# Sample score products grouped under a priority of their own, and the first head's key and query parts a step sooner

## The chip, the cores and the metric

The kernel runs on one core of one Trainium2 chip. The time is that of one execution on the device, in microseconds (us); lower is better. Below, "before" is the kernel as it stands and "after" the changed one.

## The reference: what is computed

One layer of a hybrid decoder, in float32: a half-step SwiGLU FFN, a mixing stage, a second half-step FFN, each behind RMS norms. The mixing stage runs differential attention (four heads) and an mLSTM (four heads) side by side on the same projections. There is one prompt of 512 tokens and there are 8 samples of 4 new tokens each; the samples attend to 512 past tokens that lie in 4 pages of 128 tokens each in a paged cache.

```python
proj = h @ w_in                      # 1024 -> 3592: q, k, v of attention, q, k, v, o of the mLSTM, gates
...
past_k = cache_k[l][page_table].reshape(DB, -1, H_ATT, ATT_KDIM)
...
logits = jnp.einsum('bqhcd,bkhcd->bchqk', q, k, preferred_element_type=jnp.float32) * (ATT_DQ ** -0.5)
...
p = jax.nn.softmax(logits, axis=-1)
a = p[:, 0] - lam * p[:, 1]
return jnp.einsum('bhqk,bkhd->bqhd', a.astype(v.dtype), v)
```

For a sample, keys are the 512 past ones and the 4 new ones; each head has two logit maps (`c` is 0 or 1), whose softmaxes are subtracted.

## The kernel before

**Stages.** First FFN (to about 430 us of the span), mixing stage (about 430 to 760), second FFN. All tokens, 512 + 32, stand in the free dimension, in two halves of 288 and 256 columns, with 1024 features as 8 tiles of 128 partitions. A float32 product is done as three products of rounded parts (`mm3`, L252 to L254): weight high by input high, weight high by input low, weight low by input high. So half a projection tile is 8 x 3 = 24 matmuls of 288 or 256 columns. The rounded weight parts `wh` (ScalarE, L240) and `wl` (VectorE, L241) are made from `raw` weights just before.

**Order in the mixing stage.** `mix` writes a row of projections. `run(project(...))` takes one step of every side queue (`side.step()`) after each half projection. The queues are generators: `prep` (new heads, one at a time), `attn` (blocks of 128 queries, three at a time), `ml` and `mls` (mLSTM of prompt and samples) and `smp` (attention of the samples). The order of the code is a first plan; the Tile scheduler then orders each engine's instructions by priority, which without a statement to the contrary is the place in the code, as soon as it expects operands and buffers to be ready. `tc.high_priority(offset)` moves what is written in it ahead by `offset` places; `tc.issue_after(ins)` puts it behind `ins`. Each engine then runs its list strictly in that order, and semaphores make it wait where operands are late.

**Attention of the prompt.** `attn_head(h)` adds four blocks to the `attn` queue. A block's first step, for block 0, makes the head's key parts (`key_parts`, L1237) and the first query parts (`query_parts`, L1246): rounded high and low parts `cs` and `vb` on ScalarE (L1243, L1244, L1253) and VectorE (L1255). The next step has four score matmuls (QK, L1271, `aux<-cs,vb`), the softmax, four transposes (L1297) and the products with the values (L1303).

**Attention of the samples** (`attn_samples`). The samples come in two groups of four (`g`). For each pair of pages `p` and sample `j` two pages of keys are gathered by GpSimd (`page`, L1320, into one of 7 `pgin` buffers, AHEAD = 3 pages early); each is turned by four transposes (L1346) into a PSUM tile `smp` and copied by ScalarE into `pgT` (L1347). The PSUM pool `smp` has two buffers, and one of them, `lg`, holds the logits from the first score on, so the transposes of the next page wait for the copy of the last. `scores(p, j, kT)` (L1334) multiplies one head's 128x32 queries `qz` with 256 keys, for four heads: output columns `p*256` on, partitions `32*h` on. When two (p, j) are waiting, both are multiplied: 8 matmuls, here called a score group; there are 8 of them, 4 for each `g`. Behind the last comes `ln`, 16 matmuls with the 32 new keys (L1373, `smp<-kas,qz`), then the softmax (L1388 and before) and the transposed weights (L1392), then the values' pages. GpSimd's list also holds the mLSTM's sample state: load (L1519), a copy (L1520) and store (L1586).

**End of the stage.** L1600 is the last transpose of attention output; from it `X` is scaled (L1604), gated (L1815), rounded to `h` (L1787, with its remainder L1788 on VectorE), and the out projection's second half (L252 to L254 again) multiplies it.

Of the kernel before, what the change touches and what calls it, by code (L numbers as in the profile page):

```python
# [22 lines left out]
NS = NB * NT  # L23
# [7 lines left out]
H = 4  # L31
# [12 lines left out]
PLAIN = 6  # L44
KEEP = 8

LEAD = 3
# [157 lines left out]
class _Builder:  # L205
# [1003 lines left out]
    def attn_head(self, h, k, v, side):  # L1209
        nc = self.nc  # L1210
        hd = self.hd
        kt = hd.tile([128, 4, 128], F32, name="kt")
        vt = hd.tile([128, 4, 132], F32, name="vt")
        for qb in range(4):
            side.add("attn", self.attn_block(h, qb, self.X[:, 4 + h, :], k, vt))
            if qb < 2:
                yield
# [40 lines left out]
    def attn_block(self, h, qb, q, k, vt):  # L1258
        nc = self.nc
        wk = self.wk  # L1260
        n = (qb + 1) * 128
        if qb == 0:
            self.key_parts(k)
            self.query_parts(q[:, 0:n])
            yield
        P = []
        z = wk.tile([128, 6], F32, name="z", bufs=6)
        for c in range(2):
            ps = self.ps_tile()
            for a in range(2):  # L1270
                nc.tensor.matmul(ps[:, 0:n], lhsT=self.qt[:, 2 * a + c, :], rhs=self.ks[c][:, 0:n],  # L1271
                                 start=a == 0, stop=a == 1)
# [29 lines left out]
        for kb in range(qb + 1):  # L1302
            nc.tensor.matmul(po[:, 0:128], lhsT=aT[:, kb * 128:kb * 128 + 128], rhs=vt[:, kb, 0:128],  # L1303
                             start=kb == 0, stop=kb == qb)
# [8 lines left out]
    def attn_samples(self):  # L1313
        nc = self.nc
# [10 lines left out]
        todo = [(g, 2 * p + e, j) for g in range(2) for p in range(NPG // 2) for j in range(4) for e in range(2)]  # L1325
        ahead = [page(0, 4 * g + j, pg) for g, pg, j in todo[:AHEAD]]
        dm = self.mcv("dmask")
        for g in range(2):
            lg = self.smp.tile([128, 512], F32, name="smp")
            todo_scores = []  # L1330

            def scores(p, j, kT):
                for h in range(H):
                    nc.tensor.matmul(lg[32 * h:32 * h + 32, p * 256:p * 256 + 256], lhsT=self.qz[:, 4 * g + j, h, :],  # L1334
                                     rhs=kT[:, h, :], start=j == 0, stop=j == 3, tile_position=(0, 32 * h))
            for p in range(NPG // 2):
                for j in range(4):
# [10 lines left out]
                    if len(todo_scores) == 2:  # L1348
                        while todo_scores:
                            scores(*todo_scores.pop(0))  # L1350
                    todo_scores.append((p, j, kT))
# [16 lines left out]
            ln = self.smp.tile([128, 512], F32, name="smp")  # L1368
            while todo_scores:
                scores(*todo_scores.pop(0))  # L1370
            for j in range(4):
                for h in range(H):
                    nc.tensor.matmul(ln[32 * h:32 * h + 32, 0:NS], lhsT=self.qz[:, 4 * g + j, h, :], rhs=self.kas[:, h, :],  # L1373
                                     start=j == 0, stop=j == 3, tile_position=(0, 32 * h))
            Ls = self.pg.tile([128, PAST + NS], F32, name="Ls", bufs=1)
# [574 lines left out]
```

## Time and profile before

| | |
|---|---|
| runs | 1122.38, 1123.57, 1124.5 us; median 1123.57 |
| profiled execution | 1126.08 us, of which the span is 1123.3 |
| TensorE (PE) | 1102.2 us busy, 98% of the span |
| VectorE (DVE), ScalarE (ACT), GpSimd (POOL) | 845.0, 632.5, 125.5 us busy |
| mixing stage, 430 to 715 us | TensorE busy 277.76 of 285.00 us |

A row of the timeline has the start, the length of what it groups, engine, line and operation, output and inputs, count, and in square brackets the idle time of the engine just before and what ended it. Lengths of matmuls overlap (the next one starts before the last is through), so the time that a matmul costs is read from the difference of two starts. Rows of the timeline give the matmul's form as 128*32 where 128 rows and 32 columns of the array are used; the trace has two records for each score matmul, and for a new-key one as well.

### The profile page before, as it was taken

The page shows a single profiled execution, that of the slowest core. Times are in us where ns is not written, and L with a number is a line of the kernel's source. Part 1 is how long each engine was busy: PE and PEld are TensorE (multiplying, and loading weights), DVE is VectorE, ACT ScalarE, POOL GpSimd, SP SyncE. Part 2 cuts the span into 40 slices and gives each one's busy share as a digit, 9 for nine tenths or more (in the row PEclk, how much of TensorE's full clock was granted, in tenths as well). Part 3 has the DMA queues.
Part 4 walks back from the last instruction along what each step waited for, and adds up shares of the span by engine and source line. Part 5 has one row for each costly group of instructions (what it writes and reads, how often), then busy time and mean ns, then how long its engine had stood idle before and what let it go on. Part 6 is the DMA issues. An engine that isn't in the chain of part 4 may idle for free.

```text
span 1123.3 us, 21928 instructions
## 1 busy us (share of the span) xinstructions
PE 1102.2 (98%) x8722; PEld 1063.4 (95%) x8722; DVE 845.0 (75%) x1716; ACT 632.5 (56%) x1368; POOL 125.5 (11%) x177
## 2 busy tenths in 40 slices
PE   9999999999999999999999999989999999999997
PEld 8899999999999998899889789989999999999997
DVE  5897787878675799658675478889687888786544
ACT  5844455556455657667554467776355455555444
POOL 1000000000000133420244441000000000000000
PEclk9999999999999999999999999999999999999999
DMA  9443344224246555543355546643333333242272
GB/s 265 144 126 101 116 133 130 79 66 151 71 149 178 154 146 137 185 130 90 96 159 172 174 135 208 192 158 110 113 108 123 131 101 104 81 140 90 85 211 80
DMA packets 150038, 149.47 MB, mean 133 GB/s; under 512 B 5966, under 2 KB 139062, under 8 KB 148401
## 3 DMA queue, kind: packets, MB, share of 16 engines
q1 hardware_dynamic: 135600, 100.55, 30.1%
q0 software_dynamic: 11536, 44.88, 11.9%
q10 hardware_dynamic: 2800, 2.65, 0.8%
q8 instruction: 68, 1.11, 0.4%
q14 instruction: 34, 0.27, 0.1%
HBM read 130.08 MB, written 18.51 MB: 132 GB/s over the span
## 4 chain that ended last, share of the span: by engine, by line
PE 87%; DVE 5%; ACT 3%; DMA 2%; issue 2%; POOL 0%; DVEq 0%; POOLq 0%; ACTq 0%
PE acc L252 13%; PE acc L253 13%; PE acc L254 13%; PE acc L479 6%; PE acc L477 6%; PE acc L478 6%; PE aux L477 5%; PE aux L479 5%; PE aux L478 5%; PE smp L477 2%; PE smp L479 2%; PE smp L478 2%; DVE wl L241 1%; PE smp L1346 1%; ACT wh L240 1%
## 5 line engine op out<-in xcount | busy, mean ns | idle before, releaser
L240 ACT CAST wh<-raw 128x512 fp32r<-128x512 f32 (+2 forms) x281 | 182.9, 684 | 150.2 <-PE acc L253 72.2
L241 DVE TENSOR_TENSOR wl<-raw,wh 128x512 fp32r<-128x512 f32 (+2 forms) x281 | 208.6, 768 | 47.1 <-ACT wh L240 43.5
L252 PE MATMUL acc<-ha,wh 128*128 128x256 f32 (+1 forms) x576 | 166.4, 289 | 0.0
L253 PE MATMUL acc<-ha,wh 128*128 128x256 f32 (+1 forms) x576 | 166.0, 288 | 0.0
L254 PE MATMUL acc<-ha,wl 128*128 128x256 f32 (+1 forms) x576 | 165.5, 287 | 0.0
L252 PE MATMUL acc<-h,wh 128*128 128x256 f32 (+1 forms) x552 | 163.7, 297 | 0.0
L253 PE MATMUL acc<-h,wh 128*128 128x256 f32 (+1 forms) x552 | 160.3, 291 | 0.0
L254 PE MATMUL acc<-h,wl 128*128 128x256 f32 (+1 forms) x552 | 159.5, 289 | 0.0
L252 PEld LDWEIGHTS acc<-h,wh 128*128 128x128 f32 x552 | 104.0, 188 | 7.7 <-issue 7.1
L252 PEld LDWEIGHTS acc<-ha,wh 128*128 128x128 f32 x576 | 108.9, 189 | 0.8 <-ACT wh L240 0.6
L253 PEld LDWEIGHTS acc<-ha,wh 128*128 128x128 f32 x576 | 108.9, 189 | 0.1
L254 PEld LDWEIGHTS acc<-ha,wl 128*128 128x128 f32 x576 | 108.9, 189 | 0.0
L253 PEld LDWEIGHTS acc<-h,wh 128*128 128x128 f32 x552 | 104.1, 189 | 0.7 <-issue 0.4
L254 PEld LDWEIGHTS acc<-h,wl 128*128 128x128 f32 x552 | 103.9, 188 | 0.6 <-issue 0.4
L241 DVE TENSOR_TENSOR wl<-X,wh 128x1024 fp32r<-128x1024 f32 x48 | 58.8, 1224 | 26.3 <-ACT wh L240 26.3
L479 PE MATMUL acc<-t,wl 128*128 128x272 f32 x256 | 74.3, 290 | 0.0
L477 PE MATMUL acc<-h,wh 128*128 128x272 f32 x256 | 74.2, 290 | 0.0
L479 PE MATMUL acc<-h,wl 128*128 128x272 f32 x256 | 74.1, 289 | 0.0
L477 PE MATMUL acc<-t,wh 128*128 128x272 f32 x256 | 74.0, 289 | 0.0
L478 PE MATMUL acc<-t,wh 128*128 128x272 f32 x256 | 73.8, 288 | 0.0
L478 PE MATMUL acc<-h,wh 128*128 128x272 f32 x256 | 73.7, 288 | 0.0
L240 ACT CAST wh<-X 128x1024 fp32r<-128x1024 f32 x48 | 50.4, 1050 | 25.5 <-PE aux L478 14.8
(512 smaller groups left out, 3103.2 us busy)
## 6 DMA issues: line engine op xcount, KB each, us to landing
raw<-in_ffn_w_gate_dram SPq DMA_DIRECT2D x20, 1024.0 KB
raw<-in_w_in_dram SPq DMA_DIRECT2D x28, 512.0 KB
raw<-in_ffn_w_down_dram SPq DMA_DIRECT2D x21, 512.0 KB
rawx<-in_ffn_w_up_dram SPq DMA_DIRECT2D x8, 1024.0 KB
X<-in_ffn_w_up_dram SPq DMA_DIRECT2D x8, 1024.0 KB
raw<-in_ffn_w_down_dram SPq DMA_DIRECT2D x8, 1024.0 KB
raw<-in_ffn_w_down_dram SPq DMA_DIRECT2D x21, 384.0 KB
raw<-in_w_out_dram SPq DMA_DIRECT2D x7, 1024.0 KB
```

The lines of the kernel that those rows point to most:

```text
L240: self.nc.scalar.copy(out=high, in_=src)
L241: self.nc.vector.tensor_tensor(out=low, in0=src, in1=high.bitcast(F32), op=ALU.subtract)
L252: nc.tensor.matmul(ps, lhsT=wh, rhs=xh(k0 + k), start=st, stop=False)
L253: nc.tensor.matmul(ps, lhsT=wh, rhs=xl(k0 + k), start=False, stop=False)
L254: self.last_mm = nc.tensor.matmul(ps, lhsT=wl, rhs=xh(k0 + k), start=False, stop=sp).ins
L477: nc.tensor.matmul(ps, lhsT=wh[:, k0 + k, cs], rhs=high[:, k, :], start=st, stop=False, skip_group_check=True)
L478: nc.tensor.matmul(ps, lhsT=wh[:, k0 + k, cs], rhs=low[:, k, :], start=False, stop=False, skip_group_check=True)
L479: self.last_mm = nc.tensor.matmul(ps, lhsT=wl[:, k0 + k, cs], rhs=high[:, k, :], start=False, stop=sp, skip_group_check=True).ins
L1346: nc.tensor.transpose(ps[:, h * 128:h * 128 + 128], kp[:, h * 128:h * 128 + 128], self.ident)
```

## The change

Three edits, all in the mixing stage. (1) A pair's eight score products come as one group under `tc.high_priority(offset=AHEAD_OF)`, the later (p, j) first, with start and stop flags set to match. (2) The new-key products stand under the same priority, the heads in reverse order, and the last score group is put behind them with `issue_after`. (3) Head 0's key parts and first query parts are made in `attn_head`'s first step, with an extra `yield` behind them; block 0 of the other heads makes its own as before. The number of instructions of every engine stays as it was.

```diff
@@ -43,6 +43,8 @@
 
 PLAIN = 6
 KEEP = 8
+
+AHEAD_OF = 20000
 
 LEAD = 3
 
@@ -1211,6 +1213,10 @@
         hd = self.hd
         kt = hd.tile([128, 4, 128], F32, name="kt")
         vt = hd.tile([128, 4, 132], F32, name="vt")
+        if h == 0:
+            self.key_parts(k)
+            self.query_parts(self.X[:, 4, 0:128])
+            yield
         for qb in range(4):
             side.add("attn", self.attn_block(h, qb, self.X[:, 4 + h, :], k, vt))
             if qb < 2:
@@ -1260,8 +1266,9 @@
         wk = self.wk
         n = (qb + 1) * 128
         if qb == 0:
-            self.key_parts(k)
-            self.query_parts(q[:, 0:n])
+            if h:
+                self.key_parts(k)
+                self.query_parts(q[:, 0:n])
             yield
         P = []
         z = wk.tile([128, 6], F32, name="z", bufs=6)
@@ -1329,10 +1336,15 @@
             lg = self.smp.tile([128, 512], F32, name="smp")
             todo_scores = []
 
-            def scores(p, j, kT):
-                for h in range(H):
-                    nc.tensor.matmul(lg[32 * h:32 * h + 32, p * 256:p * 256 + 256], lhsT=self.qz[:, 4 * g + j, h, :],
-                                     rhs=kT[:, h, :], start=j == 0, stop=j == 3, tile_position=(0, 32 * h))
+            def scores(todo):
+
+                with self.tc.high_priority(offset=AHEAD_OF):
+                    for p, j, kT in reversed(todo):
+                        for h in range(H):
+                            nc.tensor.matmul(lg[32 * h:32 * h + 32, p * 256:p * 256 + 256],
+                                             lhsT=self.qz[:, 4 * g + j, h, :], rhs=kT[:, h, :],
+                                             start=j == 1, stop=j == 2, tile_position=(0, 32 * h))
+                todo.clear()
             for p in range(NPG // 2):
                 for j in range(4):
                     kT = self.pg.tile([128, H, 256], F32, name="pgT", bufs=3)
@@ -1346,8 +1358,7 @@
                             nc.tensor.transpose(ps[:, h * 128:h * 128 + 128], kp[:, h * 128:h * 128 + 128], self.ident)
                         nc.scalar.copy(out=kT[:, :, e * 128:e * 128 + 128], in_=ps.rearrange("p (h k) -> p h k", h=H))
                     if len(todo_scores) == 2:
-                        while todo_scores:
-                            scores(*todo_scores.pop(0))
+                        scores(todo_scores)
                     todo_scores.append((p, j, kT))
                     if p == 1 and j == 1:
                         vps = [page(1, 4 * g + jj, 0) for jj in range(4)]
@@ -1366,12 +1377,13 @@
                     nc.gpsimd.dma_start(out=self.o[name][0].rearrange("b t h d -> (b t) h d"), in_=dst)
                     yield
             ln = self.smp.tile([128, 512], F32, name="smp")
-            while todo_scores:
-                scores(*todo_scores.pop(0))
-            for j in range(4):
-                for h in range(H):
-                    nc.tensor.matmul(ln[32 * h:32 * h + 32, 0:NS], lhsT=self.qz[:, 4 * g + j, h, :], rhs=self.kas[:, h, :],
-                                     start=j == 0, stop=j == 3, tile_position=(0, 32 * h))
+            with self.tc.high_priority(offset=AHEAD_OF):
+                for j in range(4):
+                    for h in reversed(range(H)):
+                        mm = nc.tensor.matmul(ln[32 * h:32 * h + 32, 0:NS], lhsT=self.qz[:, 4 * g + j, h, :],
+                                              rhs=self.kas[:, h, :], start=j == 0, stop=j == 3, tile_position=(0, 32 * h))
+            with self.tc.issue_after(mm.ins):
+                scores(todo_scores)
             Ls = self.pg.tile([128, PAST + NS], F32, name="Ls", bufs=1)
             z = wk.tile([128, 6], F32, name="z", bufs=6)
             f = PAST - 128
```

The changed kernel's lines are numbered otherwise: scores L1344, transposes L1358, new-key products L1383, QK L1278, `mm3` L254 to L256, pages L1327, state load, copy and store L1531, L1532 and L1598.

On TensorE, at head 0's first QK products, before (the high and low parts of the input are called h_4314, h_4315 for the first half of the tokens and h_4621, h_4622 for the second):

```order
L254 MATMUL acc<-h_4621,wl 128x256
L1271 MATMUL aux<-cs,vb 128x128 x4
L252 MATMUL acc<-h_4314,wh 128x288
L253 MATMUL acc<-h_4315,wh 128x288
L254 MATMUL acc<-h_4314,wl 128x288
L252 MATMUL acc<-h_4314,wh 128x288
L253 MATMUL acc<-h_4315,wh 128x288
L254 MATMUL acc<-h_4314,wl 128x288
L252 MATMUL acc<-h_4314,wh 128x288
L1271 MATMUL aux<-cs,vb 128x256
```

and after:

```order
L256 MATMUL acc<-h_4314,wl 128x288
L1278 MATMUL aux<-cs,vb 128x128 x4
L1358 MATMUL smp<-base,pgin 128x128 x8
L254 MATMUL acc<-h_4621,wh 128x256
L1278 MATMUL aux<-cs,vb 128x256 x2
L255 MATMUL acc<-h_4622,wh 128x256
L256 MATMUL acc<-h_4621,wl 128x256
L254 MATMUL acc<-h_4621,wh 128x256
L255 MATMUL acc<-h_4622,wh 128x256
```

The first QK products stand now behind a whole half projection that they stood ahead of, two pages' transposes follow them at once, and the second block's follow after one projection product instead of seven.

On TensorE, at the third score group, around head 1's values (`aux<-base,v` are the transposes of the values to token order), before:

```order
L1198 MATMUL aux<-base,v 128x128 x4
L1297 MATMUL aux<-base,L 128x128 x4
L1346 MATMUL smp<-base,pgin 128x128 x4
L1334 MATMUL smp<-pgT,qz 32x256 x5
L1346 MATMUL smp<-base,pgin 128x128 x4
L1334 MATMUL smp<-pgT,qz 32x256 x3
L252 MATMUL acc<-h_4621,wh 128x256
L253 MATMUL acc<-h_4622,wh 128x256
```

and after:

```order
L1200 MATMUL aux<-base,v 128x128 x2
L1358 MATMUL smp<-base,pgin 128x128 x4
L1200 MATMUL aux<-base,v 128x128 x2
L1278 MATMUL aux<-cs,vb 128x128 x2
L1344 MATMUL smp<-pgT,qz 32x256 x8
L1278 MATMUL aux<-cs,vb 128x128 x2
L1358 MATMUL smp<-base,pgin 128x128 x4
```

The group is whole, with QK products on both sides, and no transposes of a page stand within it.

On GpSimd, at the last key pages of the second group of samples, before (`cs` is the mLSTM's sample state there):

```order
L1320 DMA pgin<-in_cache_k_dram,idx 128x512 x2
L1320 DMA pgin<-in_cache_v_dram,idx 128x512 x3
L1586 DMA out_dram<-cs 128x4x128
L1320 DMA pgin<-in_cache_v_dram,idx 128x512
L1519 DMA cs<-in_state_C_dram 128x4x128
L1520 COPY cs<-ncol 128x4x2
L1320 DMA pgin<-in_cache_k_dram,idx 128x512
L1586 DMA out_dram<-cs 128x4x128
```

and after:

```order
L1327 DMA pgin<-in_cache_k_dram,idx 128x512 x2
L1327 DMA pgin<-in_cache_v_dram,idx 128x512 x4
L1327 DMA pgin<-in_cache_k_dram,idx 128x512
L1598 DMA out_dram<-cs 128x4x128
L1327 DMA pgin<-in_cache_v_dram,idx 128x512
L1531 DMA cs<-in_state_C_dram 128x4x128
```

The last key page stands right behind the four value pages, and the store and the load of a state, with its copy, stand behind it.

In the counts of the whole stage, TensorE's list changes between projection products and other work 208 times now, 196 before; the sample softmax's transposed weights (L1392) of the first group have 63 matmuls between the last scores and themselves, 24 before; and the last attention transpose (L1600) stands 24 matmuls later among the out projection's.

## The prediction

> **What bounds the kernel now.** I read the page's first part, then its chain, then a table of windows over the mixing stage, the only stage that the change reorders.
>
> ```profile
> span 1123.3 us, 21928 instructions
> PE 1102.2 (98%) x8722; PEld 1063.4 (95%) x8722; DVE 845.0 (75%) x1716; ACT 632.5 (56%) x1368; POOL 125.5 (11%) x177
> PE 87%; DVE 5%; ACT 3%; DMA 2%; issue 2%; POOL 0%; DVEq 0%; POOLq 0%; ACTq 0%
> ```
>
> ```profile
> 430.00:450.00 20.00, 18.51 (x140) 17.34 (x140) 18.27 (x76) 15.38 (x44) 9.62 (x14) 1.00 0.66 178
> ...
> 630.00:650.00 20.00, 18.14 (x179) 15.46 (x178) 10.60 (x41) 10.01 (x30) 8.06 (x10) 1.00 0.51 158
> 650.00:715.00 65.00, 65.00 (x517) 58.08 (x516) 48.70 (x149) 41.63 (x124) 17.20 (x24) 1.00 0.57 179
> sum 285.00, PE 277.76 PEld 249.94 DVE 200.12 ACT 173.10 POOL 93.47; mean PE 39.68 PEld 35.71 DVE 28.59 ACT 24.73 POOL 13.35
> ```
>
> TensorE (the first figure behind the length) is busy 98% of the span at a granted clock of 1.00, so time is won only where it stands still, or where its own stream runs less densely than it could. It stands still for 285.00 - 277.76 = 7.24 us in this stage, a fifth of it at the start, where VectorE is busy 18.27 of 20 us, and a quarter around 640. The change removes and adds no instruction and leaves SyncE's order as it is. The 7.24 us, and what interleaving costs inside busy time, are all that it can win.
>
> **The change part by part.** First the score groups. The trace has two records for each of a group's eight products, and in the new order all of them stand side by side. On TensorE's timeline of before:
>
> ```profile
> 455.43 1.07 PE L1334 MATMUL smp<-pgT,qz 128*32 128x256 f32 x16 [0.27 <-issue]
> 456.43 0.39 PE L253 MATMUL acc<-h,wh 128*128 128x256 f32 x1
> ...
> 478.26 1.05 PE L1334 MATMUL smp<-pgT,qz 128*32 128x256 f32 x10
> 479.25 0.66 PE L1346 MATMUL smp<-base,pgin 128*128 128x128 f32 x4
> 479.83 0.63 PE L1334 MATMUL smp<-pgT,qz 128*32 128x256 f32 x6
> 480.39 0.39 PE L252 MATMUL acc<-h,wh 128*128 128x256 f32 x1
> ...
> 530.88 0.48 PE L1373 MATMUL smp<-kas,qz 128*32 128x32 f32 x32
> 531.29 0.40 PE L252 MATMUL acc<-h,wh 128*128 128x288 f32 x1
> ...
> 630.57 1.05 PE L1334 MATMUL smp<-pgT,qz 128*32 128x256 f32 x10
> ...
> 644.21 0.63 PE L1334 MATMUL smp<-pgT,qz 128*32 128x256 f32 x6
> 644.77 0.44 PE L1537 MATMUL aux<-base,sm 128*128 128x128 f32 x2
> ...
> 645.28 0.83 PE L1334 MATMUL smp<-pgT,qz 128*32 128x256 f32 x9
> ...
> 646.51 0.49 PE L1483 MATMUL aux<-vt,kt 128*128 128x130 f32 x2
> ```
>
> A whole group takes 456.43 - 455.43 = 1.00 us from its start to the next work's. The split one at 478.26 takes 0.99 and 0.56 us in its two pieces (479.25 - 478.26, 480.39 - 479.83): 0.55 more. The one at 630.57 is split in the same way, after ten. The one at 644.21 takes 0.56 and, with its 32 short new-key products, 1.23; whole it would be 1.00 and, as behind the first sample group, 531.29 - 530.88 = 0.41 for the short ones, so 0.4 more. Joined, the three give 0.55 + 0.55 + 0.4 = **-1.5**, and 0 if the transposes, once put elsewhere, pay the same two changes there; the whole groups of now follow on such neighbours at 1.00, so I take the full value.
>
> [...]
>
> Second, cuts. A group put into a projection interrupts it. The nearest row is four transposes there:
>
> ```profile
> 460.89 0.29 PE L254 MATMUL acc<-h,wl 128*128 128x288 f32 x1
> 461.24 0.66 PE L1346 MATMUL smp<-base,pgin 128*128 128x128 f32 x4
> 461.65 0.38 PE L252 MATMUL acc<-h,wh 128*128 128x288 f32 x1
> 461.87 0.30 PE L253 MATMUL acc<-h,wh 128*128 128x288 f32 x1
> ```
>
> The product behind the cut takes 0.22 us until the next instead of 0.13, 0.09 more; the entry, 0.35 from 460.89 instead of 0.13, is 0.22 more, part of which may be a wait. I take 0.17 a cut, the return and a third of the entry, between 0.09 and 0.31. In the new order of the stage TensorE changes 208 times between projection products and others, 196 before. That is six more cuts: **+1.0**, from +0.5 to +1.9.
>
> Third, head 0. Its key and query parts move one step ahead in program order, and its first scores one step back:
>
> ```profile
> 436.64 0.33 PE L1271 MATMUL aux<-cs,vb 128*128 128x128 f32 x1 [0.18 <-issue]
> ...
> 438.72 0.39 PE L1271 MATMUL aux<-cs,vb 128*128 128x256 f32 x1 [0.77 <-ACT wh L240]
> ...
> 443.19 1.07 PE L1271 MATMUL aux<-cs,vb 128*128 128x384 f32 x3 [0.46 <-DVE vb L1255]
> ```
>
> and on ScalarE's:
>
> ```profile
> 435.89 2.26 ACT L240 CAST wh<-raw 128x512 fp32r<-128x512 f32 x4
> ```
>
> ScalarE rounds four weights (2.26 us) between two sets of query parts, and TensorE's in-order stream, which has the products that need these parts in front, stands 0.18 + 0.77 + 0.46 us, with some 0.1 to 0.15 us of restart behind each (it shows as a first product that takes 0.23 instead of 0.13): about 1.7 us. In after a whole half projection stands ahead of the first scores, so that they start near 439.2, 3 us later, with the parts long ready. Block 1 then follows after one product, and waits for its query parts and the restart: I allow 0.65. Gain **-1.0**, between 0 (ScalarE's queue is only shifted, and the same weights are late) and -1.7. The 24-product step goes through the attention queue everywhere; its other heads keep the same neighbours within a few products, so I cost them at nothing: it is the projections' products that hide them, and without these one such stall is 0.5 us.
>
> Fourth, the last key page of the second sample group. TensorE's row and GpSimd's rows of the timeline:
>
> ```profile
> 640.04 0.63 PE L1346 MATMUL smp<-base,pgin 128*128 128x128 f32 x4 [1.85 <-DMA pgin<-in_cache_k_dram,idx]
> ```
>
> ```profile
> 630.36 0.79 POOL L1519 DMA_DIRECT2D cs<-in_state_C_dram  x1 [1.32 <-issue]
> 631.14 1.36 POOL L1520 COPY cs<-ncol 128x8 f32<-128x8 f32 x1
> 632.67 0.99 POOL L1320 DMA_INDIRECT pgin<-in_cache_k_dram,idx  x1 [0.16 <-issue]
> ```
>
> The piece of the chain of waits (start, length, what) that ends at those transposes:
>
> ```profile
> 632.67 7.24 DMA pgin<-in_cache_k_dram,idx
> ```
>
> The page's load stands behind a state's load and a copy on GpSimd; its buffer is free when the transposes near 630.5 are done, so it goes out 2.2 us later than it could. In after it stands right behind the four value pages and ahead of the state's store and load: out near 0.3 us behind those transposes, 1.9 us earlier. Its own transposes are wanted 6.65 us behind them instead of 7.7, as one step of other work in between is gone. By 7.24 us of landing, 0.3 + 7.24 - 6.65 = 0.9 us of the stall (2.0 with the restart) stay, and less if it lands sooner, with no state's load in front of it. I take half of that: **-1.5**, from -1.0 to -2.0. What is moved behind it, the state's load and store, has a whole sample step to its use.
>
> [...]
>
> Fifth, the end of the first sample group:
>
> ```profile
> 537.05 0.91 PE L1392 MATMUL smp<-s,Ls 128*128 128x128 f32 x6 [0.55 <-DVE s L1388]
> ```
>
> TensorE waits for the softmax of sample scores. Between these and this line stand 24 products before and 63 after (39 of 0.12 to 0.13 us each, some 4.8 us more). The wait with its restart is gone: **-0.7**, and nothing comes in its place unless the scores themselves are late; from -0.7 to 0.
>
> Sixth, what the priority costs. Groups and, through the PSUM pair they share, transposes come as soon as they can be planned, and so nearer to ScalarE's copies of the transposed pages:
>
> ```profile
> 467.96 0.66 PE L1346 MATMUL smp<-base,pgin 128*128 128x128 f32 x4 [0.42 <-ACT pgT L1347]
> ```
>
> and all copies of that line (shortest, median, longest in ns):
>
> ```profile
> L1347 ACT COPY pgT<-smp x32: 562/585/614, 445.5 to 640.7; 128x512 f32<-128x512 f32 x32
> ```
>
> The copy takes 585 ns. One such wait is there now (0.42, 0.58 with restart). For two places of after I find something ahead of the copy on ScalarE: an exponential and head parts ahead of one page's, about 0.6, and other copies ahead of that of the new keys, about 0.4. For the other groups I allow 0.1 each. With 0.5 us of the present wait going: **+1.1**, from -0.4 to +4.1 (every one of eight at 0.58, less the present one).
>
> Seventh, the end of the stage. The last attention transpose (L1600) comes 24 products later, and the out projection's second half needs what follows from it:
>
> ```profile
> 706.06 0.27 PE L1600 MATMUL aux<-base,y 128*128 128x128 f32 x1
> 708.80 1.02 ACT L1787 CAST h<-X 128x256 fp32r<-128x256 f32 x3 [1.74 <-DVE X L1815]
> 710.85 0.43 DVE L1788 TENSOR_TENSOR h<-X,h 128x256 fp32r<-128x256 f32 x1
> 710.89 0.28 PE L252 MATMUL acc<-h,wh 128*128 128x256 f32 x1
> ```
>
> From that transpose to the first rounded tile it takes 708.80 + 0.34 (a third of the three) - 706.06 = 3.1 us, to the last remainder 711.28 - 706.06 = 5.2. Now 710.89 - 706.06 = 4.8 us lie between it and the first product that needs one of these tiles; in after 20 products of 0.12 and two short ones stand there, with 24 fewer some 3.1. TensorE then waits next to nothing at the first tile and a few tenths at the last, which is wanted three steps of three products, 1.1 us, after the first: **+0.35**, from 0 to 5.2 - 3.1 - 1.1 = +1.0.
>
> Sum: -1.5 + 1.0 - 1.0 - 1.5 - 0.7 + 1.1 + 0.35 = -2.25 us. The profiled execution took 1126.08 (span 1123.3 and 2.78 around it) and would take 1123.8; it stands 2.5 over the median of the runs, 1123.57, so for the median the sum gives 1121.3.
>
> **The rivals.** *The waits only move* (about 1123.8). If ScalarE's copies are what the groups wait for all through, the sixth term is its upper end, 3.0 us more, and the sum is +0.75; with half a microsecond back from fewer cuts, about no change. For it: ScalarE and VectorE are busiest where the first groups stand (15.38 and 18.27 of 20 us). Against: a copy is 0.59 us and four groups lie in windows where ScalarE is half idle (10.01 of 20).
>
> *The end of the stage turns into a wait* (1126). This one ends on the other side. With 24 products less of cover, the second half of the out projection waits for whatever its last tile takes beyond 3.1 + 1.1 = 4.2 us from the last transpose. At 5.2 us that is 1.0; from 9.2 us on it is 5.0, 4.6 more than the sum's +0.35, and the kernel is slower by over 0.2%: four microseconds of other work on VectorE or ScalarE ahead of that chain. For it: the cast waited 1.74 us for VectorE already, and the second group's sample outputs and the norm sums of the first half fall in this place. Against: ScalarE is busy 41.63 of the last 65 us and VectorE 48.70, so four microseconds in one piece are much.
>
> *It does less than it says* (1122.5). A priority cannot move a product ahead of its operands. If head 0's stall (-1.0) only moves, and the page lands 7.24 us after its issue (0.5 less), 1.5 of the sum are gone.
>
> *More comes back* (1119.6). The page is in time (0.5), head 0's whole stall goes (0.7), a cut costs only the return (0.5).
>
> **How the numbers follow.** 0.2% is 2.25 us, about what a measurement of this kernel can tell from no change; the limits are 1121.3 and 1125.8. My sum 0.47, more comes back 0.21, less than it says 0.13, the waits only move 0.09, the end of the stage 0.10. The sum's own range is 1120.3 to 1122.3; it lies at the limit, and I count a little over half of it, 0.26, as faster, since of its terms the second and sixth are costs that I put near the high side. Faster 0.26 + 0.21 + 0.02 (of the case of less) = 0.49; slower 0.10 + 0.01 (of the moved waits) = 0.11; the same 0.40. The range from 1118.3 (3.0 below the sum: the lower ends of terms three, four and six lie 0.7 + 0.5 + 1.5 = 2.7 under the values taken, that of the second 0.5) to 1124.6 (the moved waits at their upper end) leaves the slower case out.
>
> **What would show it.** All eight groups as one row of 16 of about 1.05 us on TensorE's timeline; no row of head 0's scores with a wait of over 0.4; the stall ahead of the last page's transposes under 1.0; no wait at the sample softmax; TensorE's idle time in the stage 7.24 before, about 4.5 after; no idle time ahead of the second half of the out projection over 0.5. I am wrong if several groups show waits for page copies of 0.4 or more, if the last page is still late by 1.5, or if a stall of several microseconds stands near 710.

## The result, and the profile after

The change makes the kernel slower: 1129.92 us median of 4 runs (1128.56 to 1130.69) against 1123.14 for before (4 runs, 1122.38 to 1124.5), a ratio of 1.0065 with a 95% interval of 1.0052 to 1.0078. Predicted were 1121.3, from 1118.3 to 1124.6. Ratios here and below are estimated from all runs but two slow ones on chip C (1461.63 us of e10 and 1768.22 of before, at a granted clock of 0.67 and 0.56), and are not the quotients of two medians, which would be 1.0060 here. The profiled execution of after took 1128.56, the fastest of its four, that of before 1126.08, more than any of its four timed runs, so these two traces show 2.5 us of the 6.8 between the medians; the places count here, and sizes come from the repeats further down.

The page of after, in the lines that answer to those shown of before:

```profile
span 1126.6 us, 21919 instructions
PE 1102.3 (98%) x8722; PEld 1062.2 (94%) x8722; DVE 845.8 (75%) x1716; ACT 632.5 (56%) x1368; POOL 125.0 (11%) x177
PE 86%; DVE 6%; ACT 4%; DMA 3%; issue 1%; DVEq 0%; ACTq 0%; POOLq 0%
```

and its windows over the stage (length, busy time of PE, PEld, DVE, ACT and POOL, granted clock, DMA share, GB/s):

```profile
430.00:450.00 20.00, 19.27 (x152) 18.52 (x151) 18.25 (x72) 15.72 (x43) 10.34 (x13) 1.00 0.73 207
...
630.00:650.00 20.00, 20.00 (x202) 18.38 (x195) 13.23 (x49) 11.22 (x34) 8.36 (x12) 1.00 0.61 185
650.00:715.00 65.00, 62.31 (x479) 55.27 (x478) 44.27 (x139) 37.88 (x113) 16.93 (x23) 0.97 0.54 167
sum 285.00, PE 276.79 PEld 247.22 DVE 195.67 ACT 168.50 POOL 92.01; mean PE 39.54 PEld 35.32 DVE 27.95 ACT 24.07 POOL 13.14
```

TensorE's busy total is the same within 0.1 us, and its idle time in the stage went from 7.24 to 285.00 - 276.79 = 8.21 us instead of to 4.5. It moved: the idle time at 430 to 450 fell from 1.49 to 0.73 and that at 630 to 650 from 1.86 to nothing, but 650 to 715, full before, now has 2.69, at a mean granted clock of 0.97.

I then set the two TensorE lists side by side, projection product by projection product, and took the difference in start. From 430 to 737 of before, after falls 5.8 us behind. Up to 537 it gains 5 us; between 537 and 571 it loses 6.5, then gains 1.1, and between 692 and 722 it loses 5.5.

**The first place** is the values of the first sample group. Before, a page's value products of four samples stand in one piece:

```profile
555.53 1.06 PE L1409 MATMUL smp<-pgin,saT 128*32 128x512 f32 x8
556.52 0.40 PE L252 MATMUL acc<-h,wh 128*128 128x288 f32 x1
```

In after (L1421 is the same line) QK products (L1278) stand between them:

```profile
550.59 0.64 PE L1278 MATMUL aux<-cs,vb 128*128 128x128 f32 x4
551.16 1.04 PE L1421 MATMUL smp<-pgin,saT 128*32 128x512 f32 x2
552.35 0.39 PE L1278 MATMUL aux<-cs,vb 128*128 128x256 f32 x1
552.67 1.04 PE L1421 MATMUL smp<-pgin,saT 128*32 128x512 f32 x2
553.64 0.38 PE L1278 MATMUL aux<-cs,vb 128*128 128x256 f32 x1
553.96 1.05 PE L1421 MATMUL smp<-pgin,saT 128*32 128x512 f32 x4
554.94 0.40 PE L254 MATMUL acc<-h,wh 128*128 128x288 f32 x1
```

Four products (two records each) side by side, each on 32 columns of the array, take 556.52 - 555.53 = 0.99 us together. One alone takes as long: 552.35 - 551.16 = 1.19 and 553.64 - 552.67 = 0.97; two take 0.98. So this page costs 3.14 us instead of 0.99. Over the stage, before has 9 such pieces, 9.18 us to the next work, and after 13, 13.31 us: this page is in three, the one before it (540.62) is mixed with the products of the new values, the one behind it (564.67) is cut by a transpose, and one page of the second group is cut in two as it was before. Why four that follow each other directly take no longer than one is not shown here.

**The second place** is near 702. TensorE stops in the middle of a tile of the out projection, at a product of the samples' mLSTM state:

```profile
698.77 0.29 PE L254 MATMUL acc<-h,wh 128*128 128x288 f32 x1
701.76 0.47 PE L1593 MATMUL aux<-vb,kr 128*128 128x512 f32 x1 [2.69 <-DVE vb L1589]
...
703.32 0.44 PE L254 MATMUL acc<-h,wh 128*128 128x288 f32 x1
703.56 0.44 PE L255 MATMUL acc<-h,wh 128*128 128x288 f32 x1
```

Then products stand 0.24 us apart (703.56 - 703.32) instead of 0.13: the granted clock fell to half for 3.4 us (0.50 from 702.60 to 705.80), here called a spell, which costs 1.7 us more. The operand that was waited for hangs on a weight. The chain of waits, and then ScalarE's and VectorE's timelines:

```profile
689.19 8.37 DMA raw<-in_w_out_dram
697.66 0.63 ACT wh L242
```

```profile
689.24 0.43 ACTq L1814 DMA_DIRECT2D X<-x_keep  x1
697.66 0.62 ACT L242 CAST wh<-raw 128x512 fp32r<-128x512 f32 x1 [4.18 <-DMA raw<-in_w_out_dram]
698.31 0.69 DVE L243 TENSOR_TENSOR wl<-raw,wh 128x512 fp32r<-128x512 f32 x1 [4.12 <-ACT wh L242]
...
700.93 0.68 DVE L1589 TENSOR_TENSOR vb<-vr,mixc 128x512 fp32r<-128x512 f32 x1
```

and, of before, the same reload of the residual (L1802 there):

```profile
687.32 0.37 ACTq L1802 DMA_DIRECT2D X<-x_keep  x1
```

A load of the out projection's weights, issued at 689.19, took 8.37 us to land. The reload of the residual's first half starts with it, at 689.24; before, the reload went out at 687.32 and that load at 690.51, 3.2 us later, and no engine waited for it. (That trace doesn't tell when the load landed; in the trace of b2 below, the same kernel once more, it took 5.50 us.) ScalarE's rounding waits 4.18 us for the load, VectorE's remainder behind it 4.12, and `vb`, which has nothing to do with this weight, stands behind the remainder in VectorE's list. TensorE's in-order list has its product in front, and stops.

In sum, 430 to 737, after less before, in TensorE's time: value products +4.0, cut projections +1.8, half clock +1.7, idle +1.6; scores -1.2, new keys -0.4, transposes of pages -1.3, smaller ones -0.4. That makes 5.8.

### The profile page after: what moved, and what is told of

Read it like the earlier page. It is cut to its first block, busy times and chain, and to the rows that moved or that the text cites. A ratio compares the mean times of both kernels' runs of the same rounds, so it can differ in the third digit from the quotient of the medians.

```text
span 1126.6 us, 21919 instructions
## 1 busy us (share of the span) xinstructions
PE 1102.3 (98%) x8722; PEld 1062.2 (94%) x8722; DVE 845.8 (75%) x1716; ACT 632.5 (56%) x1368; POOL 125.0 (11%) x177
## 4 chain that ended last, share of the span: by engine, by line
PE 86%; DVE 6%; ACT 4%; DMA 3%; issue 1%; DVEq 0%; ACTq 0%; POOLq 0%
PE acc L254 13%; PE acc L255 13%; PE acc L256 13%; PE acc L481 6%; PE acc L479 6%; PE acc L480 6%; PE aux L479 5%; PE aux L481 5%; PE aux L480 5%; PE smp L479 2%; PE smp L481 2%; PE smp L480 2%; ACT wh L242 1%; DMA x_ffn<-X 1%; DVE wl L243 1%
## 5 line engine op out<-in xcount | busy, mean ns | idle before, releaser
L254 PE MATMUL acc<-ha,wh 128*128 128x256 f32 (+1 forms) x576 | 165.6, 288 | 0.0
L254 PE MATMUL acc<-h,wh 128*128 128x256 f32 (+1 forms) x552 | 164.7, 299 | 0.6 <-ACT y L344 0.6
L256 PE MATMUL acc<-ha,wl 128*128 128x256 f32 (+1 forms) x576 | 164.9, 286 | 0.0
L256 PE MATMUL acc<-h,wl 128*128 128x256 f32 (+1 forms) x552 | 160.4, 291 | 0.0
L254 PEld LDWEIGHTS acc<-h,wh 128*128 128x128 f32 x552 | 104.7, 190 | 6.7 <-issue 5.4
L254 PEld LDWEIGHTS acc<-ha,wh 128*128 128x128 f32 x576 | 108.3, 188 | 0.8 <-ACT wh L242 0.6
L256 PEld LDWEIGHTS acc<-ha,wl 128*128 128x128 f32 x576 | 108.3, 188 | 0.0
L256 PEld LDWEIGHTS acc<-h,wl 128*128 128x128 f32 x552 | 104.4, 189 | 1.5 <-issue 1.2
```

What stands on the lines that cost most here:

```text
L254: nc.tensor.matmul(ps, lhsT=wh, rhs=xh(k0 + k), start=st, stop=False)
L256: self.last_mm = nc.tensor.matmul(ps, lhsT=wl, rhs=xh(k0 + k), start=False, stop=sp).ins
```

## The experiments

All ratios are to before on the same chip, with 95% intervals. Four groups of kernels ran, each on one chip, called A to D; before took 1125.97, 1122.32, 1125.13 and 1125.3 us there.

| kernel | chip | median us | ratio | interval |
|---|---|---|---|---|
| e1_head: edit 3 alone | A | 1136.5 | 1.0085 | 1.0068 to 1.0102 |
| e2_scores: edits 1 and 2 | A | 1125.75 | 1.0005 | 0.9992 to 1.0019 |
| e10_scores: the same | C | 1125.32 | 1.0000 | 0.9990 to 1.0009 |
| a2_after: all three | B | 1130.85 | 1.0078 | 1.0065 to 1.0091 |
| f1_after: the same | D | 1134.0 | 1.0081 | 1.0059 to 1.0102 |
| e3_rev: values reversed | A | 1133.59 | 1.0065 | 1.0048 to 1.0081 |
| e7_rev: the same | C | 1130.08 | 1.0050 | 1.0032 to 1.0067 |
| f2_rev: the same | D | 1131.8 | 1.0060 | 1.0042 to 1.0078 |
| e4_later: reload later | A | 1130.75 | 1.0039 | 1.0025 to 1.0054 |
| e8_later: the same | C | 1129.82 | 1.0043 | 1.0028 to 1.0059 |
| f3_later: the same | D | 1131.72 | 1.0054 | 1.0036 to 1.0072 |
| e6_repairs: both | B | 1123.88 | 1.0023 | 1.0014 to 1.0032 |
| f4_both: the same | D | 1129.72 | 1.0034 | 1.0023 to 1.0046 |
| e9_first: both, reversal in group one only | C | 1128.61 | 1.0032 | 1.0020 to 1.0043 |
| e5_scores_rev: edits 1, 2, values reversed | B | 1123.82 | 1.0012 | 1.0004 to 1.0021 |
| b2_before: before again | B | 1122.14 | 1.0002 | 0.9993 to 1.0010 |

### Which edit makes the loss

**e1_head**: before with the third edit alone.

```diff
         vt = hd.tile([128, 4, 132], F32, name="vt")
+        if h == 0:
+            self.key_parts(k)
+            self.query_parts(self.X[:, 4, 0:128])
+            yield
...
         if qb == 0:
-            self.key_parts(k)
-            self.query_parts(q[:, 0:n])
+            if h:
+                self.key_parts(k)
+                self.query_parts(q[:, 0:n])
             yield
```

> The kernel before with the third edit alone: head 0's key and query parts a step sooner, everything behind in the attention queue a step later. Theory (the step's shift does the harm: it cuts the samples' value products into more pieces of 0.98 us each, +4.1, and puts a weight load of the out projection beside the reload of the residual, a stall of 2.7 and a spell at half clock, +1.7): 1129 to 1132 us, with 13 pieces of value products where before has 9. Rival (the score groups' priority does the harm, the head's move is a gain of 1.0 as predicted): 1121.5 to 1122.5.

It is 0.85% slower by itself, about as much as all three edits in their three comparisons (0.65, 0.78 and 0.81%). TensorE's timeline (value products L1414, QK L1276, state product L1586):

```profile
443.22 0.50 PE L1276 MATMUL aux<-cs,vb 128*128 128x256 f32 x2 [2.27 <-ACT vb L1257]
...
557.37 1.04 PE L1414 MATMUL smp<-pgin,saT 128*32 128x512 f32 x2
558.57 0.39 PE L1276 MATMUL aux<-cs,vb 128*128 128x256 f32 x1
558.88 1.05 PE L1414 MATMUL smp<-pgin,saT 128*32 128x512 f32 x2
...
710.33 0.71 PE L1586 MATMUL aux<-vb,kr 128*128 128x512 f32 x1 [3.03 <-DVE vb L1582]
```

Both places of after are there, the cut values in the same 13 pieces (13.52 us) and the stall of 3.03 us near 710. A third is new, 2.27 us at head 0's second score block, for which see below. The reload starts 0.04 us behind the weight load (697.48 and 697.44). The third edit makes the loss, and the priority is not needed for it.

**e2_scores** and **e10_scores**: after without the third edit.

```diff
-        if h == 0:
-            self.key_parts(k)
-            self.query_parts(self.X[:, 4, 0:128])
-            yield
...
-            if h:
-                self.key_parts(k)
-                self.query_parts(q[:, 0:n])
+            self.key_parts(k)
+            self.query_parts(q[:, 0:n])
```

> The changed kernel without the third edit: score groups and new-key products with their priority, head 0 as before. Theory (the shift of a step does the harm): 1119.5 to 1121.5 us, the score products 1.6 us shorter in all, value products in 9 pieces as before. Rival (the priority does the harm): 1127 to 1130.

> The score groups and new-key products with priority alone, again. Theory (whole groups save 1.6 us of TensorE's time and the page stall of 2 us goes, but waits for page copies and cuts take it back): 0.999 to 1.0015 of before. Rival (the first result hides a gain behind late signals on that chip): 0.997 to 0.998.

Both are level with before, so the gain that I expected of edits 1 and 2 isn't there. The values stand in 9 pieces, and neither trace stops TensorE near 700; in e2's the reload goes out 3.2 us ahead of the load again. The score groups are whole. In e2's trace, of the fastest of its 12 runs, the stage is 0.45 us longer than before's: new keys and transposes give 1.5 back, waits and smaller pieces 1.1, but cut projections take 2.0 and value products 1.1, and the groups save nothing, since the last one takes 2.23 us. In e10's a stall of 1.64 us at 668 with its spell at half clock is in it as well. Whole groups are thus worth about what their cuts cost, and the six cuts that I put at 1.0 cost 1.6 to 2.0.

### The two places, mended one by one

**e3_rev** and **e7_rev**: after with the values of a page taken in reverse order of samples, which leaves all pages but the first in one piece each (9 pieces, as before).

```diff
             for pg in range(NPG):
-                for j in range(4):
+                for j in reversed(range(4)):
```

> The changed kernel with the samples' value products of a page written with the last sample first, so that each page's four stand together. Theory (each extra piece costs nearly a whole page's products, 0.98 us): 4 us under the changed kernel, 1125 to 1126.5. Rival (the pieces lie in time that TensorE would have waited anyway, the stall near 700 is all): 1129 to 1130.5, as the changed kernel.

> The changed kernel with the value products of a page with the last sample first, again, on a chip that shows the changed kernel's own trace without late signals. Theory (cut value products cost 4 us of the 8): 1.003 to 1.006 of before, with the stall near 700 still there. Rival (they lie in time that is lost anyway): 1.007 to 1.009.

The first missed what I expected by 7 us, and on chip A nothing more can be read from it, since after was not timed there: four stalls of 1.65 to 2.79 us stand in that trace, of which two near 443 and 457 aren't in the trace of after. On chip C, where after was not timed either, it is 0.50% slower. Here the page of the first fence is whole, and the stall near 704 stays:

```profile
555.49 1.06 PE L1421 MATMUL smp<-pgin,saT 128*32 128x512 f32 x8
...
704.01 0.47 PE L1593 MATMUL aux<-vb,kr 128*128 128x512 f32 x1 [2.21 <-DVE vb L1589]
```

**e4_later** and **e8_later**: after with the reload of the first half put behind the evacuation of the out projection's fourth tile, so that it no longer runs beside that weight load.

```diff
-                if i == 3:
-                    for k in range(0, KT, WK):
+                if i == (4 if half == 0 else 3):
+                    with ExitStack() as after:
+                        if half == 0:
+                            after.enter_context(tc.issue_after(self.last_evac))
+                        for k in range(0, KT, WK):
```

> The changed kernel with the reload of the residual (first half) issued on ScalarE's queue behind the fourth tile of the out projection, so that the fourth weight load has the DMA engines to itself. Theory (that load lands in 8.4 us instead of 4.7 because the reload runs beside it, and VectorE's list holds the last state products' operand behind that weight): the stall of 2.7 near 700 and the spell at half clock behind it go, 1125 to 1126.5. Rival (the load is late by itself or the operand waits for other work): the stall stays over 1.5 and the time is 1128.5 to 1130.5.

> The changed kernel with the reload of the residual behind the fourth tile, again. Theory (the stall near 700 with its spell at half clock costs 4 to 5 us of the 8): 1.003 to 1.005 of before, the stall there under 1 us and no spell behind it. Rival: 1.007 to 1.009.

The stall near 704 fell to 0.73 and 1.08 us, and no spell at half clock stands behind it. Of e8:

```profile
703.86 0.47 PE L1593 MATMUL aux<-vb,kr 128*128 128x512 f32 x1 [1.08 <-DVE vb L1589]
```

The values stay in 13 pieces. So the reload that runs beside the load makes the stall: on chip B the load took 8.81 us beside it (a2 below) and 6.16 with the reload behind it (e6). Both kernels are still 0.4% slower, e4 by 4 us more than I expected.

**b2_before**, **a2_after**, **e5_scores_rev**, **e6_repairs**, on one chip: before and after unchanged; e2 with the reversed values; after with both repairs.

> The kernel before itself, for a trace and a spread on the same chip as the other runs here. Theory (the changed kernels' late signals and the spells at half clock near 440 belong to the moved step): the same time as the kernel before, 0.999 to 1.001, no spell between 430 and 740, no stall over 2 us there, and TensorE's idle time in the stage 6.5 to 8 us. Rival (TensorE's signals come late by some 2 us now and then in any kernel on this chip): one or two such late signals and 9 us or more idle in this trace too.

> The changed kernel itself on the same chip. Theory: slower by 0.5 to 0.8%, with a stall of over 2 us at head 0's second block of scores (near 441) and a spell at half clock behind it, which the first trace of it happened not to have. Rival: 0.5 to 0.8% slower with the trace of the first profile (0.5 us there, 2.7 near 700, one spell near 702).

> Score groups and new-key products with priority, head 0 as before, and the value products of a page with the last sample first. Theory (a page's piece costs 0.98 us, and one page of the second sample group is cut in two in the kernel before): 1 us under the kernel with the priority alone, 0.997 to 1.000 of before. Rival: no difference to the priority alone, 1.000 to 1.002.

> The changed kernel with both repairs: value products of a page together, and the reload of the residual behind the fourth tile. Theory (cut value products, and the stall near 700 with its spell, make the loss): 0.999 to 1.002 of before. Rival (the moved step loses at its own place, by the stall near 441 and the spell behind it, and in the waits behind that): 1.003 to 1.007.

Before against itself gives 1.0002, so a difference of 0.1% can be told here. Against what I expected, b2's trace has a spell within the stage: the stall ahead of the last key page's transposes is 2.05 us there (at 638.55; 1.85 in the first trace) and 3.4 us at half clock follow. So this stall, the prediction's fourth term, can cost before a spell too. After is 0.78% slower, 0.65 at first, with its stall at the same product, now 3.12 us and with 6.8 us at half clock, the first of them within the stall. This is a2's row and its window from 704 to 708, with a granted clock of 0.50:

```profile
704.30 0.77 PE L1593 MATMUL aux<-vb,kr 128*128 128x512 f32 x1 [3.12 <-DVE vb L1589]
```

```profile
704.00:708.00 4.00, 3.70 (x15) 3.63 (x16) 3.31 (x11) 0.98 (x3) 1.36 (x2) 0.50 0.43 106
```

It stands at head 0's second block for no more than 0.56 us, so a stall there isn't needed for the loss. With both repairs 0.23% is left of 0.78%, a little over the 0.2% that I allowed (the medians, 1123.88 and 1122.32, are 0.14% apart). In e6's trace the stage is 0.75 us shorter than before's, with these two longest waits:

```profile
674.24 1.06 PE L1421 MATMUL smp<-pgin,saT 128*32 128x512 f32 x8 [1.60 <-DMA pgin<-in_cache_v_dram,idx]
...
698.29 0.47 PE L1593 MATMUL aux<-vb,kr 128*128 128x512 f32 x1 [0.89 <-DVE vb L1589]
```

The first is what the reversal itself costs: with the last sample in front, a page is wanted that was gathered last. In e5 the same wait is 2.85 us, with a spell of 6.8 us. There, without the third edit, the reversal mends one cut page alone (8 pieces, 1.3 us less than before), and e5 is 0.12% slower than before, not faster as I expected.

**e9_first**: the later reload, and the reversal in the first group only, so that no value page is wanted too soon in the second.

```diff
-                for j in range(4):
+                for j in (range(4) if g else reversed(range(4))):
```

> The changed kernel with the later reload, and the value products with the last sample first in the first sample group only. Theory (in the second group the last sample's page is the one that lands last, and to begin with it made TensorE wait 1.6 us near 674): 1 us under the kernel with both repairs, 1.000 to 1.002 of before. Rival (one cut there costs as much as the wait): 1.002 to 1.003, as that one.

It is 0.32% slower on chip C, where I expected 0.2% at most. It has no wait of 0.9 us or more near 674 or 700, but 1.76 and 1.80 us at 441 and 456, which the trace of after doesn't have, so it doesn't tell what the second group's reversal is worth.

**f1_after**, **f2_rev**, **f3_later**, **f4_both**: after, each repair alone and both, now on one chip, since the single repairs had been timed where after had not.

> The changed kernel once more, on the chip of the three kernels that follow, so that the two repairs can be told apart there. My theory (two separate losses, both made by the third edit): 1.0065 to 1.0085 of before, with 13 pieces of value products and a stall of 2 to 3 us at 700 to 706. The rival (one loss, of head 0's own place, with late signals): the same time, but the two repairs below give next to nothing.

> The changed kernel with the samples' values taken in reverse order, alone. My theory: the 4.0 us of cut value products come back, less about a microsecond of waits for a value page, so 0.2 to 0.35% under the changed kernel on this chip; the stall at 700 to 706 stays. The rival of one cause: within 0.1% of the changed kernel, or all that both repairs give.

> The changed kernel with the later reload, alone. My theory: the stall near 704 goes from 2 to 3 us to about 1, and the spell at half clock behind it goes, 3 to 5 us in all, so 0.3 to 0.45% under the changed kernel on this chip; the 13 pieces stay. The rival of one cause: within 0.1% of the changed kernel, or all that both repairs give.

> The changed kernel with both repairs. My theory: the two gains add up, to 0.5 to 0.75% under the changed kernel on this chip, so 1.001 to 1.003 of before; more than that stays on a chip with late signals at head 0's place. The rival of one cause: no more than the better of the two alone.

Against after's 1.0081, the reversal gives 0.21%, the later reload 0.27%, both 0.47%, the last two a little less than I expected (0.3 and 0.5 at least): the gains add up, as two separate causes would, though intervals of about 0.2% either way leave room. The traces say it more sharply. Value products over before: +3.6 us in f1 and in f3, -0.3 in f2 and in f4. TensorE at that state product in f1, f2, f3 and f4:

```profile
706.04 0.77 PE L1593 MATMUL aux<-vb,kr 128*128 128x512 f32 x1 [3.13 <-DVE vb L1589]
```

```profile
706.38 0.47 PE L1593 MATMUL aux<-vb,kr 128*128 128x512 f32 x1 [3.13 <-DVE vb L1589]
```

```profile
704.54 0.47 PE L1593 MATMUL aux<-vb,kr 128*128 128x512 f32 x1 [0.32 <-DVE vb L1589]
```

```profile
705.22 0.47 PE L1593 MATMUL aux<-vb,kr 128*128 128x512 f32 x1 [0.71 <-DVE vb L1589]
```

The reversal leaves the stall at 3.13 us, the later reload takes it to 0.32, and neither touches the other's place. The rival, one cause for both, falls.

**What is left** with both repairs, 0.23 to 0.34%, is not settled. In f4's trace, of the slowest of its seven runs, which is 6.4 us behind before's over the stage, two stalls with their spells at half clock (1.7 us each) make 7.3 us:

```profile
443.21 0.50 PE L1278 MATMUL aux<-cs,vb 128*128 128x256 f32 x2 [2.26 <-ACT vb L1259]
...
674.04 0.51 PE L1593 MATMUL aux<-vb,kr 128*128 128x512 f32 x1 [1.65 <-DVE C L1500]
```

The first stands in every trace with the third edit from chips A, C and D (1.76 to 2.28 us near 442) and is 0.54 to 0.56 us in after's first trace and on chip B. The second stands in the traces with the full reversal from chips A and D alone (e3, f2, f4: 1.65 to 1.67 us; 0.33 and 0.31 at that product in f1 and f3): it is what the reversal costs there. On chip B neither stands in e6's trace, whose stage isn't longer than before's, so there the rest has no place that I can name. No version that I ran beats before.

## Why the prediction was wrong, by its steps

**The step that failed** is a sentence of the third term: "The 24-product step goes through the attention queue everywhere; its other heads keep the same neighbours within a few products, so I cost them at nothing". The other heads do keep theirs within a few products, but value products depend on a neighbour exactly: a page cost 0.99 us where its four products touch and mostly 0.97 to 1.19 us a piece where they don't. A shift by one step broke up three pages (one by QK products, one by a transpose, one among the products of the new values) and made four more pieces, +4.0 us. It also put the reload on top of a weight load at the end of the stage: +2.7 us of stall and +1.7 at half clock (3.1 and 2.9 on chip B). That is 8.4 us in the first trace for a term that I put at nothing. The order of the products shows the first of these without a run: value rows of two and six stand where there were rows of eight. The second cannot be read from that order, but the trace of before has the reload 3.2 us ahead of that load, and I did not ask whether a moved step would bring them together.

The other terms, by the first trace:

- *Score groups* (-1.5): scores and new keys are 1.6 less. All eight groups are one row of 16, as said, such as

```profile
451.19 1.07 PE L1344 MATMUL smp<-pgT,qz 128*32 128x256 f32 x16
452.19 0.39 PE L254 MATMUL acc<-h,wh 128*128 128x256 f32 x1
```

- *Cuts* (+1.0, up to 1.9): +1.8. The size was off and near its upper end.
- *Head 0* (-1.0): its stalls went from 0.18 + 0.77 + 0.46 = 1.41 to 0.54 + 0.19 = 0.73, so -0.7. "No row over 0.4" failed with

```profile
439.64 0.50 PE L1278 MATMUL aux<-cs,vb 128*128 128x256 f32 x2 [0.54 <-ACT vb L1259]
```

  which is the second block, one product behind the first, for which I had allowed 0.65 with the restart. On chips A, C and D this place is the opposite of a gain: 1.76 to 2.28 us, and a spell in each of those traces.
- *Last key page* (-1.5): the stall of 1.85 is gone, about -2.0 with the restart. GpSimd now stands ready for the transposes that free the page's buffer, and the page was in time:

```profile
633.41 0.95 POOL L1327 DMA_INDIRECT pgin<-in_cache_k_dram,idx  x1 [3.74 <-PE smp L1358]
```

- *Sample softmax* (-0.7): gone, as said.
- *Page-copy waits* (+1.1): the largest are

```profile
471.88 0.66 PE L1358 MATMUL smp<-base,pgin 128*128 128x128 f32 x4 [0.70 <-ACT pgT L1359]
523.52 0.46 PE L1383 MATMUL smp<-kas,qz 128*32 128x32 f32 x32 [0.49 <-ACT pgT L1376]
618.00 0.66 PE L1358 MATMUL smp<-base,pgin 128*128 128x128 f32 x4 [0.62 <-ACT pgT L1359]
```

  and with 0.28 and 0.17 they make 2.26; before had about 0.7, so +1.6. Several waits of 0.4 or more were one of the signs that I had named for being wrong.
- *End of the stage* (+0.35): the out projection's second half doesn't wait for what follows from the last transpose, which the term was about. Further on it waits at

```profile
722.66 0.38 PE L254 MATMUL acc<-h,wh 128*128 128x256 f32 x1 [0.57 <-ACT y L344]
```

  so +0.6, a little over the 0.5 that I had named. TensorE waits there for ScalarE's copy of a finished tile (L344), which stands behind eight roundings of weights in ScalarE's list. That the size fits is luck.

These make about -1.0 us where I had -2.25. They have the right signs, and were worth little either way. Edits 1 and 2 alone, for which the sum without head 0 and the end of the stage gives -1.6 us or 0.14%, measured 1.0000 and 1.0005. So even without the failed step the forecast of a gain would have been too high, by the cuts, the page-copy waits and, in these two traces, a last score group of over 2 us.

Of the rivals, "the end of the stage turns into a wait" had the right sign and nearly the right stage, but another place: not the second half behind the last transpose, but the first half's weights behind the reload. I gave it 0.10, arguing that VectorE was free enough; the cause was a load. "A stall of several microseconds near 710" was named as what would prove me wrong, and it is what came.

## What to carry to other kernels

When a step is moved in a queue that others share, read in the order of products what stands next to every group that took less time in one piece (0.99 us for a page here, 3.14 in three), not only next to the step: count its pieces before and after, and price each by a row of one that is cut. Ask the same of transfers: a load that landed in time here (5.50 us in b2) came too late with a second one beside it (8.37 in after, 8.81 in a2), and VectorE's in-order list handed its delay (4.12 us) to work that doesn't need it, for which TensorE stood 2.69. Where TensorE stands for two microseconds, look at the granted clock behind it too: 23 of 29 such stalls here had a spell, of 1.7 us or some 3.

## What was not expected of the hardware

**A stall of two microseconds mostly cost nearly four.** Over all traces TensorE stood 29 times for 1.6 to 3.2 us between 430 and 740, and at 23 of these stalls the granted clock fell to half for 3.4 us, or for 6.8. At half clock (0.50 in after from 702.60 to 705.80) a product of 288 columns took 0.24 us instead of 0.13, so a spell of 3.4 us cost about 1.7, and one of 6.8, which began within the stall, some 3. There is no spell in these stretches without such a stall. Here is after, around its stall:

```profile
698.00:702.00 4.00, 1.31 (x10) 1.10 (x9) 3.69 (x9) 4.00 (x12) 0.69 (x1) 1.00 0.17 58
702.00:706.00 4.00, 4.00 (x20) 3.96 (x20) 2.69 (x10) 0.43 (x1) 0.81 (x2) 0.57 0.58 170
706.00:715.00 9.00, 9.00 (x70) 8.88 (x69) 4.27 (x17) 3.71 (x11) 0.00 (x0) 1.00 0.52 159
```

The stall is in the first window (1.31 us busy of 4), the half clock in the second (0.57), which is busy all through and does 20 products where the third does 31 in the same time. The length of a stall alone doesn't tell whether a spell follows: 1.64 us had one behind it in e10 (at 668.38), 2.79 us had none in e3 (at 711.03). What sets it is not shown by these traces.

**Semaphore signals that come late.** On chips A, C and D, in all ten traces of kernels with the third edit, TensorE stands 1.76 to 2.28 us at head 0's second block for ScalarE's query parts. In e8's, VectorE and ScalarE stand just before that, 1.52 and 3.21 us, for TensorE products that have ended by the trace:

```profile
440.83 0.46 DVE L1186 TENSOR_TENSOR k<-acc,r 128x288 f32<-128x288 f32 x1 [1.52 <-PE acc L254]
```

```profile
441.02 0.30 ACT L1259 CAST vb<-X 64x128 fp32r<-64x128 f32 x1 [3.21 <-PE acc L254]
```

The last product of the tile that they wait for starts at 438.71 and ends at about 439.0. In e1's and f1's traces eight of TensorE's signals come within 0.35 us after a pause of 5 us in which its rows go on. This makes the stall of head 0's second block: in e8 its products start at 442.57, 1.55 us behind the cast at 441.02, in the first trace of after at 439.64, 1.47 behind the same cast at 438.17. It falls together with five page gathers in a row on GpSimd, but the same five stand there in the first trace of after (432.26 to 437.78), where the stall is 0.54 us, and on chip B it is 0.54 and 0.56. What holds the signals was not found.
